# One pair of width tiles split earlier, and one product moved to the smaller bank pair, in a two-layer hybrid decoder step

## The chip, the cores and the metric

One core of a Trainium2 chip runs the whole step in one launch. The metric is device time in microseconds (us), the median of the runs shown. Engines: PE (matmuls), DVE (elementwise), ACT (elementwise with one input, activations), POOL (elementwise, slower), SP (issues the loads).

## The reference, cut to what matters

Two layers run over 512 prompt rows and 8 x 4 sample rows, 544 rows in all. Each layer is a mixer of four head groups and then a feed-forward block:

```python
x = x + concat([out_a, out_b, out_c, out_d]) @ p['w_out']
h2 = rmsnorm(x, p['norm2_g'])
gate, f_conv_new = causal_dwconv(st['f_conv'], h2 @ p['ffn_w_gate'], p['ffn_conv_w'])
x = x + (jax.nn.silu(gate) * (h2 @ p['ffn_w_up'])) @ p['ffn_w_down']
```

The width is 1024 (8 tiles of 128), the feed-forward width 2816 (22 blocks of 128). Everything is float32.

## The kernel before, in words

Activations lie transposed: channels on the 128 partitions, the 544 rows (`T`) along the free axis, halves of `HT` = 272. Every float32 product is made from three passes in a rounded format: each operand is split into a rounded part `h` and a remainder `l`, and PE adds h·h, l·h and h·l. ACT makes `h` with a copy, DVE makes `l` with a subtraction: L745 and L747 for weights (tiles `wh`, `wl`, three in flight each), L515 and L516 in `split` for activations.

PE's instructions run in the order in which the program writes them. On the other engines a scheduler orders them at build time. `FFN_ORDER` is the order of the feed-forward part of a layer: blocks 0 to 4, then blocks 5 to 21, in groups that end after blocks 4, 10, 16 and 21; eight `down` tiles of the group before (tile `pdn`, w_down) stand between the blocks of a group, one or two after a block. Blocks 10 and 11, and 16 and 17, follow each other with no `down` between.

- **Blocks 0 and 1** (`raw`) use the 16 un-normed tiles `xs` and multiply the norm factor `rstd` in afterwards; the norm's sum is finished inside block 0's second product.
- **Blocks 2 to 4** (`plain`) use normed tiles. `Forms.halves(kp)` makes them for the pair of width tiles kp and kp + 4: DVE norms both (`hn`, L578), ACT rounds the two halves of the first (`f1h`, `f2h`, L586) and the whole of the second (`f3h`, L515), DVE makes the remainders (`f1l`, `f2l`, L587; `f3l`, L516). Four pairs are made, all after block 0. A gate product reads the four pairs in turn.
- **Blocks 5 to 21** (`seven`) make the gate and up products of a block from seven half-size products instead of eight. A block has the PSUM tiles `pA` (three chains: f1, f4, f5), `pB`, `pD` and `pC` (the seventh product). ACT copies results to `sn[:, 0..3]`; L1759 copies `pA` after its third chain to `sn[:, 3]`. DVE's L1761 makes one half of `up` from `pA` and `sn[:, 1]`, L1764 the other from `pC` and `sn[:, 3]`, L1765 multiplies by `sl`, and L515, L516 split the result into `hdh`, `hdl`.
- **Banks.** `psmm` (tag `mm`) turns over two large buffers; `pgt`, `pup`, `pdn` and `pC` take them in turn. `ps` (tag `ps`) turns over two small ones; in the blocks 5 to 21 only `pA` takes them. A tile's first write waits for the last reader of the tile two before it in its pool.

POOL makes the sums of weights that `seven` needs (L724 to L727), copies the convolution state out (L1689, L1690) and prepares `pbf` (L800, L802).

Of the kernel before, what the change touches and what calls it, by code (L numbers as in the profile page):

```python
# [12 lines left out]
ALU = mybir.AluOpType  # L13
# [9 lines left out]
T = SEQ + ND  # L23
HT = T // 2
# [4 lines left out]
NK = DM // 128  # L29
# [385 lines left out]
def _body(ctx, tc, I, O, depth=DEPTH, dump=None):  # L415
# [6 lines left out]
    stt = dve.scalar_tensor_tensor  # L422
# [44 lines left out]
    def n5(nm, w=571):  # L467
        return p5.tile([128, w], F32, tag="w5", name=nm)
# [10 lines left out]
    def ps(nm, shape):  # L479
        return pss.tile(shape, F32, tag="ps", name=nm)  # L480

    def psmm(nm):
        return pmm.tile([128, 1024], F32, tag="mm", name=nm)
# [29 lines left out]
    def split(src, nm):  # L513
        hi, lo = nx(nm + "h", [128, T], F32R), nx(nm + "l", [128, T], F32R)
        act(hi, src, AF.Copy)  # L515
        tt(lo, src, hi.bitcast(F32), op=ALU.subtract)  # L516
        return hi, lo
# [41 lines left out]
    def xsplit(x, g):  # L559
        hi, lo = nx("xh", [128, T], F32R), nx("xl", [128, T], F32R)  # L560
        act(hi, x, AF.Copy, scale=g)
        stt(lo, x, g, hi.bitcast(F32), op0=ALU.mult, op1=ALU.subtract)
        return hi, lo
# [55 lines left out]
    def chain(o, wt, k0, xs, start=True):  # L619
        hi, lo = wt  # L620
        n = len(xs)
        for k in range(n):
            xh, xl = xs[k]
            for i, (w, x) in enumerate(((hi, xh), (hi, xl), (lo, xh))):
                mm(o, w[:, k0 + k, :], x, start=start and k == 0 and i == 0, stop=k == n - 1 and i == 2,
                   skip_group_check=not start)
            yield 0.0
# [122 lines left out]
    def wnext():  # L750
        while len(wready) < 3:
            n = len(wready)
            wprep()
            if len(wready) == n:
                break
        return wready.pop(0)

    def gemm(p, wt, xs):
        hi, lo = wt
        n = len(xs)  # L760
        for k in range(n):
            xh, xl = xs[k]
            for wi, x in ((0, xh), (0, xl), (1, xh)):
                first = k == 0 and wi == 0 and x is xh
                last = k == n - 1 and wi == 1
                w = (hi, lo)[wi][:, k, :]
                for j in range(2):
                    mm(p[:, P0 + HT * j:P0 + HT * j + HT], w, x[:, HT * j:HT * j + HT],
                       start=first, stop=last)
            if k < n - 1:  # L770
                yield 0.0
# [10 lines left out]
    def pflat(p, a=0, b=T):  # L782
        return p[:, P0 + a:P0 + b]
# [5 lines left out]
    def bs(ap):  # L789
        return ap.rearrange("p (b t) -> p b t", b=DB)  # L790
# [14 lines left out]
    def conv(pb, K, wcol, out_n):  # L805
        acc = n5("cacc")
        act(acc[:, 0:out_n], pb[:, 0:out_n], AF.Copy, scale=wcol[:, 0:1])  # L807
        for j in range(1, K):
            stt(acc[:, 0:out_n], pb[:, j:j + out_n], wcol[:, j:j + 1], acc[:, 0:out_n],  # L809
                op0=ALU.mult, op1=ALU.add)  # L810
        e = K - 1
        return acc, acc[:, e + SEQ:e + SEQ + DB * (e + DS)].rearrange("p (b s) -> p b s", b=DB)[:, :, 0:DS]
# [3 lines left out]
    def P(l, nm, a=0, b=None):  # L816
        o, n = _POFF[nm]
        return prm_t[l][:, o + a:o + (n if b is None else b)]
# [586 lines left out]
    def main():  # L1405
# [7 lines left out]
        def xk(k):  # L1413
            return xr[k // 2][:, k % 2, :]
# [33 lines left out]
        for l in range(depth):  # L1448
# [233 lines left out]
            fm = Forms(lambda k: (xk(k), P(l, "n2g", k, k + 1)))  # L1682

            def gate_in(f):
                pb = n5("pbf")
                return pb, conv_in(pb, 3, stf[:, f])

            def gate_out(f, pb, dec):
                pool.tensor_copy(sfo[:, f, 0:2], pb[:, SEQ:SEQ + 2])  # L1689
                c_ = pool.tensor_copy(sfo[:, f, 2:18].rearrange("p (b s) -> p b s", b=DB), dec[:, :, 4:6])  # L1690
                if f == PLAIN - 2:
                    held[0] = c_.ins
                acc, accd = conv(pb, 3, P(l, "fcw", 3 * f, 3 * f + 3), 560)
                sl = n5("sl", T)
                act(sl[:, 0:SEQ], acc[:, 0:SEQ], AF.Silu)  # L1695
                act(bs(sl[:, SEQ:T]), accd, AF.Silu)
                return sl

            def raw(f, first):
                p = psmm("pgt")  # L1700
                yield from gemm(p, wnext(), xs)
                pu = psmm("pup")
                gu = gemm(pu, wnext(), xs)
                if first:
                    yield next(gu)
                    nrm.finish()
                pb, dec = gate_in(f)
                tt(pb[:, 2:2 + SEQ], pflat(p, 0, SEQ), rstd[:, 0:SEQ], op=ALU.mult)
                tt(dec[:, :, 2:6], bs(pflat(p, SEQ, T)), bs(rstd[:, SEQ:T]), op=ALU.mult)
                sl = gate_out(f, pb, dec)  # L1710
                tt(sl, sl, rstd, op=ALU.mult)
                yield 0.0
                yield from gu
                tt(sl, sl, pflat(pu), op=ALU.mult)
                hid[f] = split(sl, "hd")
                yield 0.0
# [16 lines left out]
            def seven(f):  # L1733

                B11, B21, B22, N1, N2, T3, N4 = fm.parts()
                K = NK // 2
                a_ = ps("pA", [128, HT])
                b_ = psa.tile([128, HT], F32, tag="pa1", name="pB")
                d_ = psa.tile([128, HT], F32, tag="pa0", name="pD")
                sn = pd.tile([128, 4, HT], F32, tag="d5", name="sn")  # L1740
                pb, dec = gate_in(f)
                n = SEQ - HT
                w = wnext()
                yield from chain(a_, w, 0, B11)
                act(sn[:, 0], a_, AF.Copy)
                yield from chain(b_, w, K, B21)
                tt(pb[:, 2:2 + HT], b_, sn[:, 0], op=ALU.add)
                w = wnext()
                yield from chain(d_, w, 0, N1)
                act(sn[:, 1], d_, AF.Copy)  # L1750
                yield from chain(a_, w, K, N2, start=False)
                act(sn[:, 2], a_, AF.Copy)
                w = wnext()
                yield from chain(d_, w, 0, B22, start=False)
                tt(pb[:, 2 + HT:2 + SEQ], d_[:, 0:n], sn[:, 2, 0:n], op=ALU.add)  # L1755
                tt(dec[:, :, 2:6], bs(d_[:, n:HT]), bs(sn[:, 2, n:HT]), op=ALU.add)  # L1756
                sl = gate_out(f, pb, dec)
                yield from chain(a_, w, K, T3, start=False)
                act(sn[:, 3], a_, AF.Copy)  # L1759
                up = n5("up", T)  # L1760
                stt(up[:, HT:T], a_, -1.0, sn[:, 1], op0=ALU.mult, op1=ALU.subtract)  # L1761
                c_ = psmm("pC")[:, 0:HT]
                yield from chain(c_, wnext(), 0, N4)
                tt(up[:, 0:HT], c_, sn[:, 3], op=ALU.subtract)  # L1764
                tt(sl, sl, up, op=ALU.mult)  # L1765
                hid[f] = split(sl, "hd")
                yield 0.0

            for kind, i, f0, f1 in FFN_ORDER:
                if kind == "plain":  # L1770
                    yield from raw(i, i == 0) if i < RAW else plain(i)
                    if i == 0:
                        for kp in range(NK // 2):
                            fm.halves(kp)
                    elif i == RAW:
                        with tc.issue_after(fm.end.ins):
                            fm.sums()
                    continue
                if kind == "seven":
                    yield from seven(i)  # L1780
                    continue
                m, last = i, f1 == NF
                hd = [hid[f] for f in range(f0, f1)]
                if last and l + 1 == depth and m >= NK - 2:
                    if m == NK - 2:
                        yield from finale(xk, xr, nnrm, hd)
                    continue
                p = psmm("pdn")
                yield from gemm(p, wnext(), hd)
                tt(xk(m), xk(m), pflat(p), op=ALU.add)  # L1790
                if last:
                    if l + 1 < depth:
                        nx_xs.append(xsplit(xk(m), P(l + 1, "n1g", m, m + 1)))
                    nnrm.feed(m, xk(m))
                    if l + 1 == depth:
                        act(xk(m), xk(m), AF.Copy, scale=fng[:, m:m + 1])
                yield 0.0
# [51 lines left out]
```

## Time and profile before

| what | value |
|---|---|
| median of 3 runs | 1332.42 us (1330.86 to 1334.02) |
| the profiled execution's own time | 1334.97 us, 2.55 us over the median |
| its span, first to last instruction | 1333.1 us, so 1.9 us lie around it |
| mean granted TensorE clock | 0.992 |
| PE busy | 1293.0 us, 97% |
| DVE, ACT, POOL busy | 73%, 48%, 32% |

Times in the trace count from the span's start. The feed-forward part of layer 0 lies at about 279 to 650 us, that of layer 1 at about 938 to 1333 us. PE is busy nearly throughout, so the places where it waits or runs at a lower clock are what a change can win or lose. A row of a timeline gives the start, the duration, engine, line, operation, output<-inputs, and in brackets the idle time before it with what ended that. Instructions in a row overlap at their ends, so the cost of one in a full queue is the distance between two starts.

### The profile page before, as it was taken

How to read it: one execution, taken by the hardware profiler on the slowest of the kernel's cores; microseconds unless marked ns; L12 is line 12 of the kernel's file. 1: busy time of each engine (PE TensorE's matmuls, PEld its weight loads, DVE VectorE, ACT ScalarE, POOL GpSimd, SP SyncE). 2: the span in 40 equal slices, each digit the busy share in tenths (PEclk: the TensorE clock that was granted, in tenths of full speed). 3: DMA queues.
4: the chain of work that ended last, by engine and by line, in shares of the span. 5: the costliest groups of instructions: out<-in, count | busy, mean ns of one | idle time of the engine just before them, and what ended most of it. 6: DMA issues, size and time to landing. Idle time of an engine off the chain costs nothing.

```text
span 1333.1 us, 29980 instructions
## 1 busy us (share of the span) xinstructions
PE 1293.0 (97%) x12574; PEld 1242.8 (93%) x12574; DVE 978.8 (73%) x1585; ACT 634.1 (48%) x1108; POOL 429.1 (32%) x542
## 2 busy tenths in 40 slices
PE   9999999999999999999999999999999999999997
PEld 8988888998999999999998888889989999999997
DVE  6998944679778778776659977447786787787665
ACT  6446424455445445444544453235555454454444
POOL 2531310001555355353105412100133644644331
PEclk9999999999999999999999999999999999999999
DMA  7222241232223232232532222313313333332232
GB/s 280 85 67 82 81 133 42 89 101 65 71 94 102 86 113 88 86 109 77 175 119 82 78 70 75 117 49 101 90 47 93 88 110 87 97 103 86 83 97 71
DMA packets 48087, 125.61 MB, mean 94 GB/s; under 512 B 10144, under 2 KB 14432, under 8 KB 47824
## 3 DMA queue, kind: packets, MB, share of 16 engines
q1 hardware_dynamic: 47952, 123.70, 29.8%
q8 instruction: 98, 1.61, 0.5%
q14 instruction: 37, 0.30, 0.1%
HBM read 115.01 MB, written 8.67 MB: 93 GB/s over the span
## 4 chain that ended last, share of the span: by engine, by line
PE 78%; DVE 15%; ACT 3%; issue 3%; DMA 1%; DVEq 0%; SPq 0%; ACTq 0%
PE pdn L436 18%; PE pA L436 11%; PE po L436 7%; PE pD L436 7%; PE pup L436 5%; PE pB L436 4%; DVE wl L747 4%; PE pC L436 3%; PE pgt L436 3%; DVE cacc L809 3%; PE ptm L436 2%; PE pj_b L436 2%; PE pj_z L436 2%; PE pj_h L436 2%; PE pj_c L436 2%
## 5 line engine op out<-in xcount | busy, mean ns | idle before, releaser
L747 DVE TENSOR_TENSOR wl<-wr,wh 128x1024 fp32r<-128x1024 f32 (+4 forms) x218 | 266.3, 1221 | 87.2 <-ACT wh L745 85.9
L745 ACT ACTIVATE wh<-wr 128x1024 fp32r<-128x1024 f32 (+4 forms) x218 | 194.0, 890 | 197.3 <-issue 34.1
L436 PE MATMUL pdn<-hdh,wh 128*128 128x272 f32 x684 | 142.3, 289 | 7.5 <-ACT wh L745 3.0
L436 PE MATMUL pdn<-hdl,wh 128*128 128x272 f32 x684 | 141.6, 288 | 0.5 <-DVE hdl L516 0.5
L436 PE MATMUL pdn<-hdh,wl 128*128 128x272 f32 x684 | 141.2, 288 | 0.0
L724 POOL TENSOR_TENSOR s<-wr 128x512 f32<-128x512 f32 x34 | 46.8, 1376 | 232.3 <-DVE wl L747 103.9
L745 ACT ACTIVATE wh<-s 128x1024 fp32r<-128x1024 f32 x68 | 72.0, 1059 | 98.5 <-PE pdn L436 87.8
L436 PEld LDWEIGHTS pdn<-hdh,wh 128*128 128x128 f32 x684 | 107.0, 188 | 9.3 <-ACT wh L745 3.6
L436 PEld LDWEIGHTS pdn<-hdl,wh 128*128 128x128 f32 x684 | 107.4, 188 | 0.9 <-DVE hdl L516 0.9
L436 PEld LDWEIGHTS pdn<-hdh,wl 128*128 128x128 f32 x684 | 107.3, 188 | 0.0
L809 DVE SCALAR_TENSOR_TENSOR cacc<-pbf,prm,cacc 128x560 f32<-128x560 f32 x88 | 82.1, 932 | 33.1 <-ACT cacc L807 32.5
L747 DVE TENSOR_TENSOR wl<-s,wh 128x1024 fp32r<-128x1024 f32 x68 | 92.8, 1364 | 6.0 <-ACT wh L745 5.4
L1689 POOL COPY sfo<-pbf 128x2 f32<-128x2 f32 x44 | 28.5, 648 | 147.5 <-DVE pbf L1755 63.0
L1790 DVE TENSOR_TENSOR xr<-xr,pdn 128x544 f32<-128x544 f32 x62 | 44.3, 715 | 39.4 <-PE pdn L436 39.4
L725 POOL TENSOR_TENSOR s<-wr,s 128x512 f32<-128x512 f32 x34 | 63.2, 1859 | 0.9
L727 POOL TENSOR_TENSOR s<-wr 128x512 f32<-128x512 f32 x34 | 58.9, 1731 | 0.0
L807 ACT ACTIVATE cacc<-pbf,prm 128x560 f32<-128x560 f32 x44 | 33.6, 764 | 50.2 <-DVE pbf L1756 46.3
L726 POOL TENSOR_TENSOR s<-wr,s 128x512 f32<-128x512 f32 x34 | 56.9, 1674 | 1.4
L800 POOL MEMSET pbf<- 128x2 f32 x44 | 4.3, 98 | 158.6 <-DVE sq L536 153.6
L1695 ACT ACTIVATE sl<-cacc 128x512 f32<-128x512 f32 x44 | 27.6, 628 | 36.6 <-DVE cacc L809 36.4
L516 DVE TENSOR_TENSOR hdl<-sl,hdh 128x544 fp32r<-128x544 f32 x44 | 39.2, 890 | 4.5 <-ACT hdh L515 4.5
L436 PE MATMUL pA<-f5h,wh 128*128 128x272 f32 x136 | 39.5, 290 | 0.0
(635 smaller groups left out, 4210.4 us busy)
## 6 DMA issues: line engine op xcount, KB each, us to landing
wr<-w_g SPq DMA_DIRECT2D x44, 512.0 KB
wr<-w_u SPq DMA_DIRECT2D x44, 512.0 KB
wr<-w_ch SPq DMA_DIRECT2D x38, 512.0 KB
wr<-w_d SPq DMA_DIRECT2D x32, 384.0 KB
wr<-w_d SPq DMA_DIRECT2D x32, 320.0 KB
wr<-w_o SPq DMA_DIRECT2D x12, 384.0 KB
xr<-x_in SPq DMA_DIRECT2D x7, 544.0 KB
wr<-w_tm SPq DMA_DIRECT2D x8, 392.0 KB
```

Of the source, the lines that this page charges most:

```text
L436: nc.tensor.matmul(out, lhsT, rhs, **kw)
L516: tt(lo, src, hi.bitcast(F32), op=ALU.subtract)
L724: add(s12[:, lo_], u[:, lo_], u[:, hi_], op=ALU.add)
L725: add(s12[:, hi_], g[:, lo_], s12[:, lo_], op=ALU.add)
L726: add(s43[:, lo_], g[:, hi_], s12[:, hi_], op=ALU.add)
L727: add(s43[:, hi_], g[:, lo_], u[:, lo_], op=ALU.add)
L745: act(hi, r, AF.Copy)
L747: tt(lo, r, hi.bitcast(F32), op=ALU.subtract)
L807: act(acc[:, 0:out_n], pb[:, 0:out_n], AF.Copy, scale=wcol[:, 0:1])
L809: stt(acc[:, 0:out_n], pb[:, j:j + out_n], wcol[:, j:j + 1], acc[:, 0:out_n], op0=ALU.mult, op1=ALU.add)
L1689: pool.tensor_copy(sfo[:, f, 0:2], pb[:, SEQ:SEQ + 2])
L1790: tt(xk(m), xk(m), pflat(p), op=ALU.add)
```

## The change

`Forms.halves(0)`, the first pair's norm and split, is written inside block 0, ahead of its convolution, and the loop after block 0 makes only the pairs 1 to 3. In `seven`, `pC` comes from the small pool `ps` in turn with `pA`, and L1761 reads ACT's copy `sn[:, 3]` in place of `pA`. The work done is the same.

```diff
@@ raw
                 tt(dec[:, :, 2:6], bs(pflat(p, SEQ, T)), bs(rstd[:, SEQ:T]), op=ALU.mult)
+                if first:
+                    fm.halves(0)
                 sl = gate_out(f, pb, dec)
@@ seven
-                stt(up[:, HT:T], a_, -1.0, sn[:, 1], op0=ALU.mult, op1=ALU.subtract)
-                c_ = psmm("pC")[:, 0:HT]
+                stt(up[:, HT:T], sn[:, 3], -1.0, sn[:, 1], op0=ALU.mult, op1=ALU.subtract)
+                c_ = ps("pC", [128, HT])
@@ after block 0
-                        for kp in range(NK // 2):
+                        for kp in range(1, NK // 2):
                             fm.halves(kp)
```

**DVE's queue in block 0 of layer 0.** From the gate's scaling (L1708, L1709) on; `cacc` is the convolution, `hn` to `f3l` the pairs, `sl` and `hdl` the block's result. Before:

```order
L1709 TENSOR_TENSOR pbf<-pgt,rstd 128x8x4
L809 SCALAR_TENSOR_TENSOR cacc<-pbf,prm_119,cacc 128x560 x2
L747 TENSOR_TENSOR wl<-wr,wh 128x1024
L1711 TENSOR_TENSOR sl<-sl,rstd 128x544
L1714 TENSOR_TENSOR sl<-sl,pup 128x544
L516 TENSOR_TENSOR hdl<-sl,hdh 128x544
L578 SCALAR_TENSOR_TENSOR hn<-xr,prm_119,rstd 128x544 x2
```

and now:

```order
L1709 TENSOR_TENSOR pbf<-pgt,rstd 128x8x4
L578 SCALAR_TENSOR_TENSOR hn<-xr,prm_119,rstd 128x544 x2
L809 SCALAR_TENSOR_TENSOR cacc<-pbf,prm_119,cacc 128x560
L587 TENSOR_TENSOR f1l<-hn,f1h 128x272
L587 TENSOR_TENSOR f2l<-hn,f2h 128x272
L809 SCALAR_TENSOR_TENSOR cacc<-pbf,prm_119,cacc 128x560
L516 TENSOR_TENSOR f3l<-hn,f3h 128x544
L747 TENSOR_TENSOR wl<-wr,wh 128x1024
L1713 TENSOR_TENSOR sl<-sl,rstd 128x544
```

The five instructions of pair 0 now stand before the split of the next weights and the block's result, and no longer behind `hdl`. After `hdl` the queue begins with the `hn` of pair 1. Lines from 1709 on have moved by two.

**PE's queue where block 11 follows block 10, and at the second `down` after block 11**, with the engines that a wait names. Before:

```order
L436 MATMUL pC<-f5h,wl 128x272
L436 MATMUL pA<-f1h,wh 128x272
...
L436 MATMUL pdn<-hdh,wh 128x272 [waits DVE_49,Activation_49]
L436 MATMUL pdn<-hdh,wh 128x272
L436 MATMUL pdn<-hdl,wh 128x272 x2
L436 MATMUL pdn<-hdh,wl 128x272 x2
```

and now:

```order
L436 MATMUL pC<-f5h,wl 128x272
L436 MATMUL pA<-f1h,wh 128x272 [waits Activation_49]
...
L436 MATMUL pdn<-hdh,wh 128x272 [waits Activation_49]
L436 MATMUL pdn<-hdh,wh 128x272
L436 MATMUL pdn<-hdl,wh 128x272 x2
L436 MATMUL pdn<-hdh,wl 128x272 [waits DVE_49]
```

The order of the matmuls is the same throughout. Block 11's `pA` has gained a wait on ACT (the copy L1759 of block 10, the last reader of that buffer now); the `pdn` has lost a wait on DVE at its first matmul and has one at its fifth, for `wl`.

## Rows read from the trace of the kernel before

**Rows 1.** The page: the chain that ended last, shares of the span.
```profile
PE 78%; DVE 15%; ACT 3%; issue 3%; DMA 1%; DVEq 0%; SPq 0%; ACTq 0%
```

**Rows 2.** Waits of PE, whole span: us in total, times, longest.
```profile
PE pdn L436 <- ACT wh L745: 3.0, 3, 1.1
PE pgt L436 <- DVE f1l L587: 2.7, 4, 0.9
PE pdn L436 <- DVE up L1764: 2.6, 4, 0.8
```

**Rows 3.** Busy time by stretch: stretch, length, engines, granted clock, DMA share, GB/s.
```profile
313.00:315.00 2.00, 2.00 (x9) 1.93 (x9) 1.61 (x3) 0.79 (x2) 0.00 (x0) 0.50 0.00 0
```

**Rows 4.** PE's timeline: block 2's gate and up products begin, layers 0 and 1.
```profile
303.28 0.29 PE L436 MATMUL pgt<-f1h,wh 128*128 128x272 f32 x1
...
315.51 0.42 PE L436 MATMUL pup<-f1h,wh 128*128 128x272 f32 x1
...
961.96 0.29 PE L436 MATMUL pgt<-f1h,wh 128*128 128x272 f32 x1
...
974.21 0.43 PE L436 MATMUL pup<-f1h,wh 128*128 128x272 f32 x1
```

**Rows 5.** DVE's timeline from block 0's gate on, layer 0.
```profile
289.28 1.64 DVE L809 SCALAR_TENSOR_TENSOR cacc<-pbf,prm,cacc 128x560 f32<-128x560 f32 x2 [0.89 <-ACT cacc L807]
292.25 1.23 DVE L747 TENSOR_TENSOR wl<-wr,wh 128x1024 fp32r<-128x1024 f32 x1 [1.34 <-ACT wh L745]
...
297.22 1.47 DVE L578 SCALAR_TENSOR_TENSOR hn<-xr,prm,rstd 128x544 f32<-128x544 f32 x2
298.61 0.68 DVE L1708 TENSOR_TENSOR pbf<-pgt,rstd 128x512 f32<-128x512 f32 x1
...
300.44 0.43 DVE L587 TENSOR_TENSOR f1l<-hn,f1h 128x272 fp32r<-128x272 f32 x1
...
301.15 0.79 DVE L809 SCALAR_TENSOR_TENSOR cacc<-pbf,prm,cacc 128x560 f32<-128x560 f32 x1
301.86 0.72 DVE L516 TENSOR_TENSOR f3l<-hn,f3h 128x544 fp32r<-128x544 f32 x1
302.50 1.47 DVE L578 SCALAR_TENSOR_TENSOR hn<-xr,prm,rstd 128x544 f32<-128x544 f32 x2
...
313.27 0.73 DVE L516 TENSOR_TENSOR f3l<-hn,f3h 128x544 fp32r<-128x544 f32 x1
```

**Rows 6.** Timelines of PE, then DVE: two `down` tiles after blocks 19 and 11, layer 0.
```profile
590.93 0.41 PE L436 MATMUL pdn<-hdh,wh 128*128 128x272 f32 x2
591.18 0.41 PE L436 MATMUL pdn<-hdl,wh 128*128 128x272 f32 x2
...
596.23 0.49 PE L436 MATMUL pdn<-hdh,wh 128*128 128x272 f32 x2 [0.61 <-DVE up L1764]
...
591.49 0.95 DVE L747 TENSOR_TENSOR wl<-wr,wh 128x768 fp32r<-128x768 f32 x1
...
595.66 0.42 DVE L1764 TENSOR_TENSOR up<-pC,sn 128x272 f32<-128x272 f32 x1
...
455.89 0.49 PE L436 MATMUL pdn<-hdh,wh 128*128 128x272 f32 x2 [1.01 <-ACT wh L745]
...
455.32 0.42 DVE L1764 TENSOR_TENSOR up<-pC,sn 128x272 f32<-128x272 f32 x1
```

**Rows 7.** Timelines of PE, then ACT: block 17 begins, layer 0.
```profile
540.21 0.29 PE L436 MATMUL pA<-f1h,wh 128*128 128x272 f32 x1
...
540.14 0.38 ACT L1759 ACTIVATE sn<-pA 128x272 f32<-128x272 f32 x1
```

**Rows 8.** Line L1765: ns of one (min/median/max), starts; and the page's group L725.
```profile
L1765 DVE TENSOR_TENSOR sl<-sl,up x34: 710/720/1072, 361.2 to 1293.4; 128x544 f32<-128x544 f32 x34
...
L725 POOL TENSOR_TENSOR s<-wr,s 128x512 f32<-128x512 f32 x34 | 63.2, 1859 | 0.9
```

**Rows 9.** Busy time in the blocks 5 to 21 of both layers (346-430, 430-640, 1005-1090, 1090-1300).
```profile
sum 589.00, PE 580.99 PEld 578.69 DVE 440.93 ACT 287.66 POOL 265.84; mean PE 145.25 PEld 144.67 DVE 110.23 ACT 71.92 POOL 66.46
```

## Prediction

> **What bounds the kernel now.** I read the chain that ended last first: PE holds 78% of it [rows 1]. So an engine's work counts only where PE waits for it. Second, the waits of PE [rows 2], which show where that is in the stretches that the change touches: the product `pgt` waits for DVE's remainder `f1l`, four times, and `pdn` waits three times for ACT's `wh` and four times for L1764. Third, timelines at these places. All the rest of the program keeps its order and is taken as unchanged.
>
> *Place one, block 2's gate product.* It is the first to read the normed pairs. It begins at 303.28 and the up product at 315.51: 12.23 us, and 12.25 in layer 1 [rows 4]. One pass of two halves takes 0.25 us (590.93 to 591.18 [rows 6]), and a product has 24 passes, so 6.0 us would do. 6.2 us are lost in each layer. DVE's queue shows why: the four pairs all stand behind block 0's result, the first `hn` begins at 297.22 and the last `f3l` at 313.27, without a gap [rows 5]. PE eats the pairs as they come. In the last of the product the clock is also down: 0.50 of full speed from 313 to 315 [rows 3].
>
> *Place two, the second `down` tile of a pair.* After block 19 the first begins at 590.93 and the second at 596.23, 5.30 us for 18 passes of 0.25 (4.50): 0.8 lost, where the wait shows 0.61. It starts 0.15 us after the end of L1764 (595.66 + 0.42 = 596.08), which reads `pC` [rows 6]. `pC` stands two tiles before in the large pool, so the `down` tile gets its buffer only when DVE has come to L1764. The weights are there: the `wl` that stands before it began at 591.49 and took 0.95. The three waits put down to ACT's `wh` are the same thing: at 455.89 the start is again 0.15 us after L1764's end (455.32 + 0.42 = 455.74) [rows 6]. So there are seven such waits, 3.0 + 2.6 = 5.6 us as shown [rows 2], and about 0.19 more in each by starts: 6.9 us.
>
> **The change part by part.**
>
> *Pair 0 moved ahead of the convolution.* By starts a pair costs DVE 1.39 (two `hn`) + 0.71 (`f1l`, `f2l`) + 0.64 (`f3l`) = 2.74 us [rows 5]. It goes in where DVE stood idle for 0.89 us ahead of the convolution's two steps and 1.34 ahead of the `wl` at 292.25 [rows 5], 2.23 together; the other 0.5 at most delays that `wl`, whose weights PE first reads at 303.28 [rows 4], ten microseconds later. Nothing there is on the path, so this costs nothing. ACT's three copies of the pair go between the convolution's first step and the next weights, ahead of nothing that PE reads before block 2. If that cover were gone (PE close behind the weights), the cost would be the 0.5.
>
> What is left behind 297.22, up to the last `f3l`: three pairs less that `f3l` itself, 3 x 2.74 - 0.64 = 7.58; L1708, L1709 and a `wl`, 1.83 (298.61 to 300.44); a second `wl`, 1.1 (1.23 as in the row, less the 0.1 by which rows overlap); two convolution steps of 0.71, 1.42; L1711 and L1714, of `f3l`'s shape, 1.28 [rows 5]; and about 0.4 for which the second `wl` waits, because its buffer comes free only when block 1's product ends at 303.28. That is 13.6: the last `f3l` begins at 310.8 in place of 313.27 and ends 0.73 later, at 311.6. The pass with `f3l` and the one with the weights' `wl` follow, 0.5 us, so the up product begins at 312.2 in place of 315.51. Gain 3.3 us a layer; layer 1 has the same rows shifted and the same 12.25, so 6.6 in all. PE still waits some 2.9 us in each: DVE still makes three pairs in the time. Of the 3.3, 2.5 come from the shorter queue and 0.8 from the clock, if it does not fall. Afterwards DVE's queue follows PE (the next weights are freed by the product's end), so the shift is passed on; POOL's sums of weights hang on block 3 and shift with it. What is late next is again `f1l` and `f3l`, of the last pair.
>
> *`pC` to the small pool.* The `down` tiles now turn over two buffers alone, and the tile two before is an older `down` that has long been added. The seven waits go: -6.9. What is late next there: the weights, which were ready at 592.4 against 595.4, when the tile would now begin [rows 6]. So I take all of it; the lower bound is half, if DVE, which is about 5 us behind PE at these places, then is late somewhere else.
>
> *The new wait of `pA`.* `pA` and `pC` share two buffers, so `pA` takes the same one in every block and must wait until ACT's L1759 has read the block before. With a `down` in between that is long past. Where blocks follow directly (10 to 11 and 16 to 17, four places) it is not: L1759 runs 540.14 to 540.52, while `pA` began at 540.21 [rows 7]. 0.31 late plus the 0.15 from release to start [rows 6] is 0.46, four times 1.8 us. What is queued behind the waiting matmul is all of PE, so this is paid in full. Bounds: 0, if ACT comes to the copy earlier, and 3, if the copy is a further 0.3 late each time.
>
> *L1761 reads the copy in place of `pA`.* The copy is done before DVE comes to it (DVE is late there), so it waits for nothing new. It now reads two tensors from SBUF. The nearest row that does is L1765, 0.72 as a rule but up to 1.07 [rows 8], so each may cost 0.35 more, 34 times 12 us of DVE at most. DVE idles for 589.0 - 440.9 = 148 us in these blocks [rows 9], 4.4 a block. I take nothing.
>
> The Trainium skill speaks against this edit (SBUF — State Buffer, section "Who interferes with whom"): a DVE instruction with both inputs in SBUF contends with a GpSimd one that reads SBUF, and the loser is blocked for the whole instruction, while one with an input from PSUM does not contend. The spread of L1765 [rows 8] agrees; by that rule the 34 instructions join those that are stretched, and the sum stays the same as long as the idle time covers it.
>
> Sum: -6.6 - 6.9 + 1.8 = -11.7. The profiled execution's own time of 1334.97 (span 1333.1 and 1.9 around it) would become 1323.3. It stands 2.55 over the median of the runs, so for the median 1332.42 - 11.7 = **1320.7 us**.
>
> **The rivals.**
>
> - *The clock still falls.* For: PE still waits, from about 307 to 312, and the fall of before came after some six microseconds of such waits. Against: the sparse stretch is shorter by half and the waits fewer. If it falls at about 312, for a stretch like the one of before (2 us at 0.50 [rows 3], with its edges some 3.3), half of that is lost: up to 1.6 us a layer. Time 1322 to 1324. The Trainium skill (TensorE: Matmul & The Clock Gate, "What's actually happening") says that the chip's window runs freely and is not tied to the kernel's start; by that rule the fall may come in one execution and not in the next.
> - *The wait at `pdn` is only passed on*, DVE's lateness showing at the next tile. For: DVE is the late engine there. Against: after each of these tiles DVE has nothing to do until PE ends it, and 148 us idle in all [rows 9]. With nothing left of the 6.9: 1332.42 - 6.6 + 1.8 = 1327.6; with half, 1324.2.
> - *Slower: L1761 and POOL's sums block each other.* Place: every block from 5 on. Price: up to one POOL sum, 1.86 us [rows 8], for each of 34. It decides once a block loses more than its 4.4 us of idle DVE time, or when POOL's sums come so late that ACT's copy, queued behind the split of a sum, is late too and `pA` waits for it. If it reached PE in half the blocks: 17 x 1.86 = 32, less 11.7: 1352. Against: the idle time, and that L1765 is stretched by 0.35 at most.
> - *The change doesn't do what it says*: not so here, since the order of the queues shows both the earlier pair and the lost and gained waits.
>
> **How the numbers follow.** My forecast, all terms within a microsecond or two: 0.66. The clock falls still: 0.17. Passed on, half or all: 0.12. Both gains lost to something that I don't see, about as before: 0.02. Slower: 0.03. The range takes in the second and the third: up to 1327.6, and down to 1317.0, by 1.8 for a `pA` that doesn't wait and 1.9 for the spread of the runs. The measurement can tell about 0.2%, 2.7 us, from no change. Faster by more than that (under 1329.7) are the first three: 0.94, of which I keep 0.92; within it 0.05; slower 0.03.
>
> **What would show it.** In the changed profile: pair 0's `hn` at about 288.3 and block 2's up product at about 312.2, 9 us after its gate product; no `pdn` that waits for L1764 or for a long finished `wh`; a `pA` that waits some 0.3 to 0.5 us for ACT's copy in four places; L1761's longest at 0.8 or so. Wrong would be: a wait at block 2 as long as now, waits of `pdn` under another name, or `pA` waits at more than four places.

## The result and the profile after

The changed kernel took **1322.5 us** (median of 4 runs, 1320.67 to 1324.78) beside 1332.61 for the kernel before: ratio 0.9928, 95% interval 0.991 to 0.9946. Run again later, with more rounds, it gave 0.993 (0.9917 to 0.9942). It is faster by about 9.5 us, 0.7%. The forecast of 1320.7 was 1.8 us low and the range held the time. The profiled execution took 1321.02 us (span 1319.2, mean clock 0.995), 13.95 less than the profiled one of before: that pair flatters the change, and why is the main thing that the experiments had to add. L1761 of the kernel before is now L1763, L1759 is L1761, L1764 is L1766, L1765 is L1767 and L1729 is L1731.

Waits of PE in the profile after, whole span (total, times, longest):

```profile
PE pdn L436 <- ACT hdh L515: 1.6, 2, 0.8
...
PE pgt L436 <- DVE f1l L587: 1.0, 2, 0.5
...
PE pA L436 <- ACT sn L1761: 0.8, 4, 0.2
...
PE pgt L436 <- DVE f3l L516: 0.7, 2, 0.4
```

`pdn` waits neither for `up` nor for `wh` any more; seven waits of [rows 2] are gone. The four forecast waits of `pA` for ACT's copy are there. The `hdh` row was there before (1.9, 2, 1.1).

**Place one.** PE's timeline, block 2's gate product and the up product after it, layer 0:

```profile
302.66 0.28 PE L436 MATMUL pgt<-f1h,wh 128*128 128x272 f32 x1
...
309.41 0.40 PE L436 MATMUL pgt<-f1l,wh 128*128 128x272 f32 x1 [0.51 <-DVE f1l L587]
...
311.03 0.52 PE L436 MATMUL pgt<-f3l,wh 128*128 128x272 f32 x2 [0.37 <-DVE f3l L516]
...
311.63 0.29 PE L436 MATMUL pup<-f1h,wh 128*128 128x272 f32 x1
```

From 302.66 to 311.63 are 8.97 us where it was 12.23 [rows 4]; in layer 1, 955.52 to 964.49, 8.97 again. Some 2.9 us a layer, by starts, are still lost to waits (8.97 less the 6.03 of a product without one). DVE's timeline of the same stretch, to be read against [rows 5]:

```profile
287.68 1.47 DVE L578 SCALAR_TENSOR_TENSOR hn<-xr,prm,rstd 128x544 f32<-128x544 f32 x2
289.07 0.80 DVE L809 SCALAR_TENSOR_TENSOR cacc<-pbf,prm,cacc 128x560 f32<-128x560 f32 x1
...
291.84 1.21 DVE L747 TENSOR_TENSOR wl<-wr,wh 128x1024 fp32r<-128x1024 f32 x1
293.69 0.72 DVE L1713 TENSOR_TENSOR sl<-sl,rstd 128x544 f32<-128x544 f32 x1 [0.64 <-ACT sl L1696]
...
296.60 1.48 DVE L578 SCALAR_TENSOR_TENSOR hn<-xr,prm,rstd 128x544 f32<-128x544 f32 x2
...
310.26 0.72 DVE L516 TENSOR_TENSOR f3l<-hn,f3h 128x544 fp32r<-128x544 f32 x1
```

Pair 0 fills the idle time ahead of `wl`, which even came at 291.84 instead of 292.25. The last `f3l` begins at 310.26 instead of 313.27.

**Place two.** PE and then ACT where block 11 begins:

```profile
435.35 0.39 PE L436 MATMUL pA<-f1h,wh 128*128 128x272 f32 x1 [0.18 <-ACT sn L1761]
435.58 0.29 PE L436 MATMUL pA<-f1l,wh 128*128 128x272 f32 x1
434.93 0.37 ACT L1761 ACTIVATE sn<-pA 128x272 f32<-128x272 f32 x1
```

Passes of one half follow each other by 0.125 us at the full clock, so by starts this place loses 0.34 at the first pass and 0.10 at the next: 0.44. The other three lose 0.44, 0.46 and 0.46.

### The profile page after: what moved, and what is told of

It reads as the page before. It is cut to its first block, busy times and chain, and to the rows that moved or that the text cites. A ratio compares the mean times of both kernels' runs of the same rounds, so it can differ in the third digit from the quotient of the medians.

```text
span 1319.2 us, 29967 instructions
## 1 busy us (share of the span) xinstructions
PE 1286.0 (97%) x12574; PEld 1237.9 (94%) x12574; DVE 982.9 (75%) x1585; ACT 637.0 (48%) x1108; POOL 430.2 (33%) x542
## 4 chain that ended last, share of the span: by engine, by line
PE 81%; DVE 12%; ACT 4%; issue 2%; DMA 1%; DVEq 0%; SPq 0%; ACTq 0%
PE pdn L436 19%; PE pA L436 11%; PE po L436 8%; PE pD L436 7%; PE pup L436 5%; PE pB L436 4%; PE pgt L436 4%; PE pC L436 3%; DVE wl L747 3%; PE ptm L436 2%; PE pj_b L436 2%; PE pj_z L436 2%; PE pj_h L436 2%; PE pj_c L436 2%; DVE cacc L809 2%
## 5 line engine op out<-in xcount | busy, mean ns | idle before, releaser
L747 DVE TENSOR_TENSOR wl<-wr,wh 128x1024 fp32r<-128x1024 f32 (+4 forms) x218 | 259.7, 1191 | 89.5 <-ACT wh L745 88.2
L724 POOL TENSOR_TENSOR s<-wr 128x512 f32<-128x512 f32 x34 | 49.2, 1448 | 264.6 <-DMA wr<-w_u 165.6
L809 DVE SCALAR_TENSOR_TENSOR cacc<-pbf,prm,cacc 128x560 f32<-128x560 f32 x88 | 78.1, 888 | 31.3 <-ACT cacc L807 30.7
L747 DVE TENSOR_TENSOR wl<-s,wh 128x1024 fp32r<-128x1024 f32 x68 | 89.6, 1318 | 7.3 <-ACT wh L745 6.9
L1689 POOL COPY sfo<-pbf 128x2 f32<-128x2 f32 x44 | 33.6, 763 | 100.1 <-ACT pbf L1725 40.8
L725 POOL TENSOR_TENSOR s<-wr,s 128x512 f32<-128x512 f32 x34 | 65.2, 1917 | 0.9
L726 POOL TENSOR_TENSOR s<-wr,s 128x512 f32<-128x512 f32 x34 | 54.5, 1603 | 2.6 <-DVE wl L747 1.2
L515 ACT ACTIVATE hdh<-sl 128x544 fp32r<-128x544 f32 x44 | 28.9, 656 | 28.2 <-DVE sl L1767 21.9
```

The lines of the kernel that those rows point to most:

```text
L724: add(s12[:, lo_], u[:, lo_], u[:, hi_], op=ALU.add)
L725: add(s12[:, hi_], g[:, lo_], s12[:, lo_], op=ALU.add)
L726: add(s43[:, lo_], g[:, hi_], s12[:, hi_], op=ALU.add)
L747: tt(lo, r, hi.bitcast(F32), op=ALU.subtract)
```

## The experiments

Every run is compared with the kernel before on its own chip (medians of 1333.3 to 1333.8 there). e1 to e4 ran together, e5 to e8, and e9 to e11. The edits are shown against the changed kernel, cut to the lines that differ; `@@` stands for what is left out.

### e1: the pair alone

```diff
-                stt(up[:, HT:T], sn[:, 3], -1.0, sn[:, 1], op0=ALU.mult, op1=ALU.subtract)
-                c_ = ps("pC", [128, HT])
+                stt(up[:, HT:T], a_, -1.0, sn[:, 1], op0=ALU.mult, op1=ALU.subtract)
+                c_ = psmm("pC")[:, 0:HT]
```

> Only the first part of the change: pair 0 of the slabs is normed and split ahead of block 0; the seventh half product stays in the large pool, the up-product sum reads the middle product's copy in SBUF as before. Theory (the two parts add): the pair is worth 3.3 us a layer, 6.6 together, so about 1326; with the wait of block 4's up product for L1729, 0.5 to 0.7 a layer in the kernel before, gone as it went in the whole change, about 1324.7. The seven waits of pdn for the up tile stay (6.9 us in all), there is no wait of pA for ScalarE's copy, and the longest instruction of L1763 stays near 0.44 us. Rival (the pair's gain needs the other part, because the down tile's wait falls in the same stretch): under 3 us gained, above 1329.

1328.2 us, ratio 0.9957 (0.9941 to 0.9974): 5.7 gained, where 6.6 was the forecast for this part; the runs can't tell these two apart. Block 2's gate product lasts from 303.17 to 312.14, 8.97 as in the whole change. Six waits of `pdn` for `up` or `wh` are there (before: seven). The theory that the pair's gain doesn't need the other part holds. The wait of block 4's up product went in layer 1 and stayed in layer 0 (0.7), of which under e11.

### e2: the bank alone

```diff
@@ raw
-                if first:
-                    fm.halves(0)
@@ after block 0
-                        for kp in range(1, NK // 2):
+                        for kp in range(NK // 2):
```

> Only the second part: all four slab pairs after block 0 as in the kernel before; the seventh half product in the second small bank and ScalarE's copy taken from it. Theory: the seven waits of pdn (6.9 us) go, the four new waits of pA come (4 x 0.45 = 1.8), so about 1327.5, a gain of 5.1. The gate products of block 2 keep their 3.6 us a layer of waiting for the slabs, and block 4's up product keeps its wait for L1729 near 0.5 us. The longest instruction of L1763 is above 0.44 us here too if its two SBUF operands, and not the order of the slabs, stretch it. Rival (pdn's wait is passed on to the next matmul): within 2 us of the kernel before.

1327.75 us, ratio 0.9955 (0.994 to 0.997): 5.9 gained, 5.1 forecast. No `pdn` waits for `up` or `wh`, and four waits of `pA` are there, 0.8 shown as in the whole change: nothing was passed on. Block 4's up product, expected to keep its wait, did not wait in either layer, of which under e11. The two parts alone make 11.6, each uncertain by about 2 us; together they gave 9.6. They add within that.

This run shows one thing more. The waits of `pgt` at block 2 are those of before (`f1l`: 2.7, 4, 0.9), and yet the product took less, since the clock did not fall. The stretch 313 to 315 (last columns: clock, DMA share, GB/s), to be read against [rows 3]:

```profile
313.00:315.00 2.00, 2.00 (x15) 1.77 (x15) 1.56 (x3) 1.18 (x3) 0.00 (x0) 1.00 0.00 0
```

It lasted from 303.23 to 314.61, 11.38, and 11.40 in layer 1. So of the 12.23 in the profile of before 0.85 was the lower clock, and only 2.4 of the 3.26 gained were the pair's.

### e3: the copy's wait taken out

```diff
-                c_ = ps("pC", [128, HT])
+                c_ = psmm("pC")[:, 0:HT] if f + 1 in (11, 17) else ps("pC", [128, HT])
```

> The changed kernel, but at blocks whose successor is 11 or 17 (the four places where pA of the next block waited for ScalarE's copy at a group's end) the seventh product goes to the large pool. Theory: the four waits of pA for L1761 (0.44 to 0.46 each, 1.8 in all) go, and no wait of pdn comes in their place: about 1.8 below the changed kernel, 1320.7 where that runs at 1322.5. Rival (the wait moves to the next tile of the large pool): no difference, and a new wait of pdn or pgt at these four places.

1321.44 us, ratio 0.9912 (0.989 to 0.9933), against 0.9928 and 0.993 for the changed kernel. The four waits are gone, where the blocks 11 and 17 begin in either layer, and the rival's new wait of `pdn` or `pgt` isn't there; the one wait that came, 0.7 of block 4's up product in layer 0, is the toss-up shown under e11. The 1.8 us are thus shown in the trace; the runs' interval is too wide to show them in the time.

### e4: the sum reads PSUM again

```diff
-                stt(up[:, HT:T], sn[:, 3], -1.0, sn[:, 1], op0=ALU.mult, op1=ALU.subtract)
+                stt(up[:, HT:T], a_, -1.0, sn[:, 1], op0=ALU.mult, op1=ALU.subtract)
```

> The changed kernel, but the up-product sum on VectorE (L1763) reads the first half product from PSUM, so that the small bank comes free only when that instruction is done. Theory: the bank's release is what decides at the four group ends: pA of the next block now waits for VectorE, some 2 us longer at each, so about 8 us slower than the changed kernel; the longest instruction of L1763 falls back to about 0.44 us, since it no longer has two SBUF operands. Rival (the release is early enough either way): no difference in the time, and pA's wait at the four places stays near 0.45 us.

1333.17 us (10 runs), ratio 1.0001 (0.9986 to 1.0016): the small bank with its reader on DVE is worth nothing, the whole gain of the change is lost. PE's waits:

```profile
PE pA L436 <- DVE up L1763: 8.5, 4, 2.1
```

2.1 us at each of the four places, 7.7 more than with ACT's copy. The theory said 8 slower; it was 9.7 by the two ratios, 10.7 by the medians. In the profile the clock adds to the waits: after two of the four, both in layer 0, it was granted at half speed, 1.2 GHz, and after the two of layer 1, as long, at full speed, 2.4 GHz. The two stretches after such waits:

```profile
439.00:442.00 3.00, 3.00 (x15) 3.00 (x15) 2.00 (x3) 0.94 (x2) 0.00 (x0) 0.50 0.00 0
1096.50:1099.50 3.00, 3.00 (x26) 3.00 (x25) 2.27 (x3) 1.11 (x3) 0.00 (x0) 1.00 0.00 0
```

A wait of 2 us can cost some 1.5 more behind it (the passes from 439 on lose 0.10 each until 442.3), and it is not sure to.

Line L1763's instruction, ns of one (min/median/max), in the profile after and here:

```profile
L1763 DVE SCALAR_TENSOR_TENSOR up<-sn x34: 427/435/1532, 354.2 to 1278.6; 128x272 f32<-128x272 f32 x34
L1763 DVE SCALAR_TENSOR_TENSOR up<-pA,sn x34: 426/429/435, 355.1 to 1288.4; 128x272 f32<-128x272 f32 x34
```

The second operand in SBUF is what lets it be stretched, by up to 1.1 us; e1 (436 at most) and e2 (1534) say the same. What stretches it is a sum of POOL that is under way. In the profile after, 14 of the 34 took 1.52 to 1.53 us, and each of them began 0.9 to 1.1 us into a POOL sum (L725 or L726); the other 20, at 0.44 at most, began beside none. In e4 14 of the 34 also began 0.9 to 1.1 us into such a sum, and took 0.43. One of each kind, first after, then e4, each row from that engine's timeline:

```profile
448.58 2.27 POOL L725 TENSOR_TENSOR s<-wr,s 128x512 f32<-128x512 f32 x1
449.63 1.52 DVE L1763 SCALAR_TENSOR_TENSOR up<-sn 128x272 f32<-128x272 f32 x1
452.63 2.27 POOL L725 TENSOR_TENSOR s<-wr,s 128x512 f32<-128x512 f32 x1
453.67 0.43 DVE L1763 SCALAR_TENSOR_TENSOR up<-pA,sn 128x272 f32<-128x272 f32 x1
```

### e5: block 2 without the slabs

```diff
-RAW, PLAIN = 2, 5
+RAW, PLAIN = 3, 5
@@ after block 2
-                    elif i == RAW:
+                    elif i == 2:
```

> The changed kernel, with block 2 computed like blocks 0 and 1 from the unnormed tiles (its two products read xh and xl, VectorE scales the result), so that the normed slabs are first needed by block 3; the sums of the forms start where they started. Theory (what is late next is the last slab pair, 2.9 us a layer on the gate product of block 2): these waits go in both layers, 5.8 us in all, about 1316.7 where the changed kernel runs at 1322.5. Rival (VectorE is full there: block 2 adds 1.6 us a layer to its queue by the rows of L1708, L1709 and L1713, and the queue has under 2 us idle between the first slab pair and the last): part of it comes back as waits of pup, pgt or pA further on, 2 to 4 us gained, with waits for DVE wl, sl or f5l in blocks 3 to 5.

1330.63 us, ratio 0.9982 (0.9966 to 0.9999): 7 slower than the changed kernel by the two ratios. The waits for the slabs (the normed and split tiles of the pairs) are gone, as the theory said, but more came back than even the rival allowed:

```profile
PE pup L436 <- ACT pbf L1726: 7.1, 2, 3.6
...
PE pup L436 <- DVE pbf L1709: 2.0, 2, 1.0
```

DVE's queue from 308 to 322 has no gap but 0.79, then carries the forms (the sums `fu`, `fv` and their splits `f4`, `f5`, which the blocks from 5 on read) and the convolution of block 3 behind the extra scaling of block 2. Block 3's last `cacc` is done at 336.8, ACT's `sl` waits for it, the copy of block 4's gate (L1725, L1726) stands behind `sl` and a `wh` on ACT until 339.07, and block 4's up product, which by its row waited for that copy, begins at 339.12, 3.5 us late. Behind that wait the clock was 0.50 for some 3 us in layer 0 and 5 in layer 1. The extra scaling, 1.6 us a layer by the rows named in the expectation, is not the largest part of this. DVE now makes the forms while POOL makes its sums, and four of DVE's instructions took 1.10 us longer each in either layer, 4.4 us a layer. DVE's timeline, then POOL's:

```profile
326.56 1.53 DVE L607 TENSOR_TENSOR fv<-hn 128x272 f32<-128x272 f32 x1
328.01 1.81 DVE L516 TENSOR_TENSOR f4l<-fu,f4h 128x544 fp32r<-128x544 f32 x1
329.75 1.53 DVE L602 TENSOR_TENSOR fv<-hn,fu 128x272 f32<-128x272 f32 x1
331.20 1.52 DVE L607 TENSOR_TENSOR fv<-hn 128x272 f32<-128x272 f32 x1
326.30 1.49 POOL L724 TENSOR_TENSOR s<-wr 128x512 f32<-128x512 f32 x1
```

In the profile of the changed kernel these forms are done by 326.4 in layer 0, none of L602 and L607 takes over 0.43 and no `f4l` over 0.72, and POOL's first sum begins at 330.74. Had DVE not lost the 4.4, the copy that block 4's up product waits for could have been done near 334.7, before the product was due at 335.4 (an estimate, from 339.07 less 4.4). No run parts the two causes.

### e6: one `down` tile later in the last group

```diff
-            k = -(-len(todo) // max(n - 1 - j, 1))
+            k = -(-len(todo) // max(n - 1 - j + (f1 == NF), 1))
```

> The changed kernel, but in the last group of each layer one down tile of the group before stands behind block 21 instead of ahead of block 20, so that the first down tile of the last group comes 4.5 us later. Theory: the wait of that tile for block 21's hdh and hdl, 1.6 us a layer (0.99 + 0.51 + 0.10), goes: 3.2 us below the changed kernel, about 1319.3. Rival (VectorE and ScalarE are then behind with the weights or with x, so that the wait moves to wh, wl or x): within 1 us of the changed kernel.

1320.1 us, ratio 0.9911 (0.9882 to 0.9941). No wait for `hdh` or `hdl` is left, and nothing new stands elsewhere but the toss-up at block 4's up product (0.7, once): the 3.2 us are there in the trace. The time fell by 2.4 against 1322.5, in line with the theory and, by the intervals, no proof of it.

### e7: two pairs ahead

```diff
@@ raw
-                    fm.halves(0)
+                    fm.halves(0), fm.halves(1)
@@ after block 0
-                        for kp in range(1, NK // 2):
+                        for kp in range(2, NK // 2):
```

> The changed kernel, with the second pair of width tiles too normed and split ahead of block 0's convolution (two pairs early, two after). Theory (VectorE's queue is the limit between 286 and 311 us, and only its idle time, 1.8 us in three gaps, can still be filled): the last slab pair comes at most 1.4 us earlier a layer, 0 to 2.8 us below the changed kernel, 1319.7 to 1322.5. Rival (block 0's activation and the release of its up tile come some 3 us later, and a product of block 1 or 2 waits for that or for its weights): slower than the changed kernel by 1 to 6 us, with new waits of pup or pgt for wl or sl ahead of 303 us.

1317.18 us, ratio 0.9888 (0.9862 to 0.9913), below the expected 1319.7. All waits of block 2 for slabs are gone (the gate product takes 6.03 us, 304.66 to 310.69); in their place the up product of block 1 waits 0.41 in each layer for L1716 of block 0, 0.65 by starts: 2.9 less 0.65, 2.25 a layer. Both halves of the expectation missed. DVE's timeline shows what:

```profile
294.59 1.22 DVE L747 TENSOR_TENSOR wl<-wr,wh 128x1024 fp32r<-128x1024 f32 x1
295.73 0.72 DVE L1713 TENSOR_TENSOR sl<-sl,rstd 128x544 f32<-128x544 f32 x1
...
308.83 0.73 DVE L516 TENSOR_TENSOR f3l<-hn,f3h 128x544 fp32r<-128x544 f32 x1
309.46 0.72 DVE L1716 TENSOR_TENSOR sl<-sl,pup 128x544 f32<-128x544 f32 x1
```

L1713 no longer waits: the 1.8 us of gaps are filled. Block 1's L1716 now stands behind the last `f3l` and no longer ahead of it, another 0.63. And PE arrives 0.65 later, so that it needs the slabs later. I had counted the gaps alone.

### e8: e3, e5 and e6 together

> The three further edits together: block 2 unnormed, the last group's order, and the seventh product in the large pool where the next block begins a group's end. Theory (they concern different waits and add): 5.8 + 3.2 + 1.8 = 10.8 us below the changed kernel, 1311.7; with block 4's up product not waiting. Rival (VectorE is full in blocks 2 to 5 and returns part): 1314 to 1318.

1323.85 us, ratio 0.9938 (0.992 to 0.9957): no better than the changed kernel. Both waits of e5 are there unchanged (7.1 and 2.0), and so are the four stretched instructions of DVE beside POOL's sums in either layer, so e5's loss ate what e3 and e6 give.

### e9: the best version, e3, e6 and e7 together

> The changed kernel with three further edits together: two slab pairs ahead of block 0's convolution (it alone gave 1317.2), the last group's order (1320.1 alone), and the seventh product in the large pool at the four group ends (1321.4 alone). Theory (three different waits, none of them moved by another): 5.3 + 2.4 + 1.1 below 1322.5, about 1313.7; by the waits in the profile (2.9 less 0.65 a layer, 1.6 a layer, 1.8 in all) 4.5 + 3.2 + 1.8 = 9.5, about 1313.0. Rival (one edit shifts VectorE and brings a wait back): above 1315.

**1310.85 us**, ratio 0.9837 (0.9821 to 0.9854), 13.1 below the changed kernel in the same rounds (e11), where 9.5 was expected. In the feed-forward parts one wait of PE over 0.1 us is left in each layer (the final norm behind them waits 0.5 once, as in the kernel before):

```profile
PE pup L436 <- DVE sl L1716: 0.9, 2, 0.4
```

By the ratios it is 12.4 (against e11's 0.993). The sum of 9.5 lacks two things that the profiles of e7 and e9 show: POOL's L724 begins more than a microsecond after DVE's weight split there (330.19 against 328.94), so that the toss-up described under e11, up to 0.75 a layer, is off; and there is hardly a wait left behind which the clock could fall, as it did in e11's profile for 1.5 us. That these two make the whole rest was not shown.

### e10: three pairs ahead

> The changed kernel with three pairs ahead of block 0's convolution. Theory (with two pairs the up product of block 1 already waits 0.4 us for VectorE's L1716 of block 0, and there is no idle time of VectorE left ahead of it): a third pair puts 2.5 to 3 us more in front of L1716, the up product of block 1 waits some 3 us a layer, and the last slab pair, which nothing waits for with two pairs, gives nothing back: 5 to 6 us slower than two pairs, near the changed kernel, 1321 to 1324, with the clock falling after the wait in some executions. Rival (L1716 stays ahead of the third pair in VectorE's order): as two pairs, 1317.

1321.79 us, ratio 0.9918 (0.9902 to 0.9933): 4.0 slower than two pairs by the two ratios, 4.6 by the medians, which are of two chips. L1716 of block 0 now stands behind the third pair's `hn`, and the up product of block 1 waits for it:

```profile
PE pup L436 <- DVE sl L1716: 3.6, 2, 1.8
...
PE pup L436 <- DVE sl L1731: 1.3, 2, 0.7
```

The first wait is 1.8 and not 3, since only a part of the third pair got ahead of L1716; the second is the toss-up described next. By starts they are 1.4 and 0.86 more than in e7, twice each, 4.5 in all. Of these 2.8 are the third pair's and 1.7 the toss-up, of which no run shows that the third pair brings it. Of the numbers tried, one to three, two is the best.

### e11: the changed kernel again

> The changed kernel again, unaltered, on the chip and in the rounds of the best version. Theory (what the change is worth does not depend on the chip or the day): 0.991 to 0.9946 of the kernel before; in the two layers the wait of block 4's up product for L1731 is there wherever GpSimd's L724 begins ahead of VectorE's weight split by any amount (GpSimd near 1.3 us, VectorE above 2.1), and absent where VectorE begins first (1.23 and 2.3). Rival (the wait depends on the change's order, not on that race): absent in both layers, as in the first profile of the changed kernel.

1323.94 us, ratio 0.993 (0.9917 to 0.9942). In its profile the clock did fall behind block 2's shortened waits, to 1.2 GHz, in layer 0:

```profile
313.60:317.20 3.60, 3.60 (x19) 3.60 (x18) 2.54 (x4) 2.39 (x4) 0.89 (x2) 0.53 0.06 10
```

The passes there lose 1.5 us together. In the first profile of the same program it stood at 1.00 there, and so it did in both layers of e1, e3, e4 and e6, which have these waits too: one fall at twelve places. With the waits of before it fell at two of four (both layers of before, neither of e2).

Block 4's up product waited for L1731 in layer 0 and not in layer 1, in one execution of one program. DVE's weight split, POOL's sum and, where it waited, PE, first layer 0, then layer 1, each row from that engine's timeline:

```profile
334.47 2.15 DVE L747 TENSOR_TENSOR wl<-wr,wh 128x1024 fp32r<-128x1024 f32 x1 [0.24 <-ACT wh L745]
334.26 1.28 POOL L724 TENSOR_TENSOR s<-wr 128x512 f32<-128x512 f32 x1
340.05 0.36 PE L436 MATMUL pup<-f1h,wh 128*128 128x272 f32 x1 [0.44 <-DVE sl L1731]
...
987.47 1.23 DVE L747 TENSOR_TENSOR wl<-wr,wh 128x1024 fp32r<-128x1024 f32 x1
987.51 2.33 POOL L724 TENSOR_TENSOR s<-wr 128x512 f32<-128x512 f32 x1
```

Who begins first keeps its speed and the other takes 0.9 to 1.1 us longer. In eight profiles (before, after, e1 to e4, e10, e11) that makes sixteen such meetings: POOL first in eight, with DVE at 2.1 to 2.4 and a wait of 0.44 to 0.67 each time; DVE first in eight, at 1.23, without a wait. Several are decided by 0.01 to 0.03 us, and in two the record has the same start for both. The Trainium skill says this of a DVE instruction with two SBUF inputs beside a GpSimd one that reads SBUF (SBUF — State Buffer, section "Who interferes with whom": the loser is blocked, and the order of issue decides); the trace agrees, and shows that the order can differ between the layers of one execution. e11's theory, that the race decides and not the change's order, holds: its rival, no wait in either layer, did not come. e6's layer 1 does not fit the simple form: POOL's row begins at 984.10, 0.6 ahead of DVE's `wl`, and yet DVE took 1.22 and POOL 2.98. There a `cacc` of DVE had begun at 984.00 and DVE had no gap until the `wl`, so DVE was first after all.

## Why the prediction was right, point by point

- **Pair 0 ahead.** Foreseen: its `hn` at 288.3, the up product of block 2 at 312.2 and 9 us after the gate product. Measured: 287.68, 311.63, 8.97. The whole stretch lay 0.6 earlier in this execution. That the fill of the idle time costs nothing held: `wl` was not later. What is late next was `f1l` and `f3l` of the last pair, as said, for the forecast 2.9 us.
- **The seven `pdn` waits.** Forecast 6.9; in the trace the first passes of these tiles lost 6.8 by starts before, 7.3 with the pass behind each, and nothing now. e2 alone gave 5.9 net of the `pA` waits, against 5.1 forecast and 5.5 by the trace.
- **The `pA` waits.** Forecast four times 0.46; measured 0.44, 0.44, 0.46, 0.46, 1.8 in all, as forecast. e3 took them out, and no other wait of the two pools came.
- **L1763.** Forecast: each stretched by 0.35 at most, nothing on the path. This bound, from L1765's longest of 1072 ns [rows 8], was wrong: up to 1.1 us, in the 14 that began beside a POOL sum, mean 0.88 (30.0 us for 34) instead of 0.43, 15 us more of this line, and L1767 reached 1440 ns. The mechanism was the one that the prediction named, and its size three times the bound. DVE's busy time as a whole rose by 4.1 us only (978.8 to 982.9), since other lines were stretched less. The zero held, since the idle time of [rows 9] covered it: the rival in which DVE and POOL hold each other up and PE waits did not come here. In e5, where such meetings stood ahead of a copy that PE waits for, they lie on the way to a loss of 7 us. POOL's L725 rose from 1859 to 1917 ns only.
- **Not priced.** Block 4's up product waited 0.52 and 0.49 for L1729 before, not at all in the profile after, and that looked like 1.5 us of gain by starts. It is the toss-up shown above. Whether the change shifts its odds is open. The wait for block 21's `hdh` fell by 0.27 in layer 0 alone.
- **The step that was mis-sized: "0.8 from the clock, if it does not fall"**, counted in full in each layer. The profile of before had a fall in block 2 of both layers, but e2's, with the same waits, has none (11.38 and 11.40 instead of 12.23 and 12.25). And after the change it can still fall (e11, 1.5 us). So this is not 1.6 us of sure gain but what one execution had and another not. Without it the sum is 2 x 2.5 + 6.9 - 1.8 = 10.1, and 9.3 to 10.1 was measured. The mean clocks point the same way: 0.993 over 38 executions of the kernel before beside e1 to e11 (one of 5978 us left out), 0.994 over the nine of the changed kernel, where the profiled pair has 0.992 and 0.995. A mean clock does not say where it fell, so how often it falls in block 2 is known from the profiles alone. The first rival, that the clock still falls, came true in one of them (e11, layer 0). The Trainium skill (TensorE: Matmul & The Clock Gate, section "What's actually happening") says that the chip's window runs freely and is not tied to the kernel's start; that the same waits are followed by a fall in one layer and not in the other (e4, e11) agrees with it.

For the profile against the profile: 3.26 + 3.28 for place one, 7.3 for `pdn`, less 1.8, plus 1.5 and 0.27 are 13.8 of 13.95.

## What to carry to other kernels

Price a change by the waits that it takes away and not by the lower clock that one profiled execution had behind them: here the waits made 10.3 us by the traces (2 x 2.4 + 7.3 - 1.8), where 9.3 to 10.1 was measured, and the clock another 1.7 in the one pair of profiles. A small bank pair pays only if its reader is early: with ACT's copy as the reader the four waits cost 0.45 each by starts, with DVE's sum 2.4, and with the lower clock behind them the whole gain. When a queue is full, fill its gaps (two pairs ahead: 5 us more) and stop when an instruction that frees a buffer is pushed back (three: 2.8 of waits). When work is moved, look at what the other engine does then: in e5 DVE's forms came to lie beside POOL's sums, and that alone cost DVE 4.4 us a layer.

## What the runs showed of the hardware that was not expected

- DVE's 128x272 instruction with both inputs in SBUF took over 1500 ns in 14 of 34 cases, each begun while a POOL sum ran, and 436 at most in the others; with one input in PSUM it never took over 436, though 14 of 34 began beside such a sum too (e4).
- A meeting of DVE's 128x1024 subtraction with POOL's 128x512 sum cost the later one 0.9 to 1.1 us (DVE from 1.23 to 2.15 or more, POOL from 1.28 to 2.3), and in four of eight profiles (e1, e3, e4, e11) the order was not the same in both layers.
- Waits of 2.1 us were followed by half the clock at two of four places (e4), and the same pattern of waits in block 2 by half the clock in the profile of before and by the full clock in e2's. With the shorter waits of the changed kernel it fell at one of twelve places.
